# Snapping four kinds of pieces of a hand-written instruction order to the time steps of a triangular inverse, in a two-layer trunk on one core

## The chip, the core and the metric

The kernel runs on one core of a Trainium2 chip. A core has five engines with one in-order queue each: PE (TensorE, matrix products), DVE (VectorE), ACT (ScalarE), POOL (GpSimd) and SP (SyncE, which here issues nearly all DMAs). The metric is the device time of one execution in microseconds (us); lower is better. Times are medians of several executions. A profile is one further execution, recorded by the hardware profiler.

## The reference

Two layers are applied to 640 tokens (128 prompt tokens and 512 latent tokens, five blocks of 128) of width 1024. Layer A is a chunked gMLP mixer; layer B is a bidirectional gated DeltaNet with eight heads. All arithmetic is fp32. What the change touches is layer B:

```python
proj = h @ w_in                                   # q, k, v, the gate z, and the decay and beta columns
qkv = silu(short_conv(qkv, conv_w))
q = l2norm(q) * D_K ** -0.5 ; k = l2norm(k)
# per head and direction, chunks of tokens:
A = where(tril_strict, (k*beta) @ k.T * decay, 0)
u, w = triangular_solve(I + A, [v*beta, k*beta*exp(gcum)])
def step(S, ...):                                 # the scan over chunks
    v_new = u - w @ S
    o = (q*exp(gcum)) @ S + qk @ v_new
    S = S * exp(g_last) + k_dec.T @ v_new
o = o_forward + flip(o_backward)
o = o * rsqrt(mean(o**2) + eps) * norm_g
y = (o * silu(z)) @ w_out
```

## The kernel before

Layer B works head by head, and the work of several heads overlaps. Each kind of work is a Python generator that issues a few instructions and yields; what is issued between two yields is called a piece here. The kinds are:

- `project_head` and `project_z`: one 128-wide block of the projection, 17 pieces. A piece is one step of the contraction: three matrix products into the PSUM tile `pp` (lines 235, 236 and 237, since each fp32 operand is split into a high and a low part). They fill PE wherever nothing else is due. The weights' split is `whi` (a cast on ACT, line 230) and `wlo` (line 231).
- `conv`: the short convolution of one block (DVE line 848, tile `cacc`), ended by lines 851 (ACT) and 853 (DVE).
- `post_k`, `post_q`, `post_v`: after the convolution. `post_v` transposes v on PE (line 240) in two goes, four 128x128 blocks and then one, into the PSUM tile `px`, and ACT copies each to `nat` (line 938). `post_q` squares q on ACT and sums on PE against a column of ones (line 869).
- `chunk`: 40 pieces that build and invert the triangular matrices of one, two and two token blocks (three groups per head). PE products (lines 964, 1002, 1017, 1028, 1029, 1047, 1056, 1057, 1063, 1073) stand in every second piece from the seventh on, and in the piece after each a DVE or ACT instruction turns the PSUM result into the next operand: `TU` (lines 1004 on DVE, 1032 on ACT), `Y` (1022, DVE), `U` (1038, ACT), `T` (1050, ACT), `G` (1075, ACT), `A` and `M` (974, 982, DVE).
- `scan`: 24 pieces per head, one unit per direction and block. Products with the state `S` (line 1112, tile `ps`), then `r` on DVE (1115) and `o` on ACT (1118) or DVE (1120), then products with `G` (1125, 1126), then the new state and the sum `o` on DVE (1134, 1140).
- `norm_o`, `gate_z`: `gate_z` transposes the output `o` back on PE into `px` (line 240; four blocks and then one, for each of two halves of a head), and DVE multiplies it onto the gate `z` (line 1213).

`px` has one PSUM buffer, `ps` two, `pt` (the inverse's) three and `pp` two. A second tile in the only `px` buffer can be written once the reader of the first is done.

`stages` gives every piece list a start and an end in units of one head (about 80 us), and `turns` spreads its pieces evenly between them, sorts all pieces by time, and by place in the list where times are equal. The three groups of `chunk` start four of their own steps apart, and a step is `CSTEP / 4` = 0.0225 of a head, so that the inverse's pieces of all groups lie on one grid and the PE products of all three groups fall on the same steps. `scan` (24 pieces over a whole head), `post_q` (7), `post_v` (5) and `gate_z` (4) lie at times off this grid. PE and SP take their instructions exactly in this order (`manual_schedule`); the orders of DVE, ACT and POOL follow from it by a scheduler.

## Time and profile before

| what | value |
| --- | --- |
| median of 3 runs | 1356.4 us (1355.96 to 1357.52) |
| the profiled execution | 1356.03 us, of it the span from first to last instruction 1354.2 us |
| PE busy | 1282.5 us (95%) |
| DVE busy | 875.7 us (65%) |
| ACT busy | 578.7 us (43%) |
| POOL busy | 502.0 us (37%) |
| mean granted PE clock | 0.99 |

Layer B's loop over heads runs from about 505 us to 1245 us of the span, and layer B's output projection from there on. Numbers of a row in the timeline are its start and its length in us, then engine, line, operation, the tiles written and read, shapes and count; in square brackets stands how long the engine had been idle before it, and what ended that. Matmuls are pipelined: one starts before the modelled end of the one before it.

### The profile page before, as it was taken

How to read it: one execution, taken by the hardware profiler on the slowest of the kernel's cores; microseconds unless marked ns; L12 is line 12 of the kernel's file. 1: busy time of each engine (PE TensorE's matmuls, PEld its weight loads, DVE VectorE, ACT ScalarE, POOL GpSimd, SP SyncE). 2: the span in 40 equal slices, each digit the busy share in tenths (PEclk: the TensorE clock that was granted, in tenths of full speed). 3: DMA queues.
4: the chain of work that ended last, by engine and by line, in shares of the span. 5: the costliest groups of instructions: out<-in, count | busy, mean ns of one | idle time of the engine just before them, and what ended most of it. 6: DMA issues, size and time to landing. Idle time of an engine off the chain costs nothing. (4 is left out here: it accounts for less than half of the span.)

```text
span 1354.2 us, 22812 instructions
## 1 busy us (share of the span) xinstructions
PE 1282.5 (95%) x8773; PEld 1137.3 (84%) x8773; DVE 875.7 (65%) x1655; ACT 578.7 (43%) x1352; POOL 502.0 (37%) x503
## 2 busy tenths in 40 slices
PE   7999999999999999888999999999999999999996
PEld 4688999999997887778888898999899898887785
DVE  4654744444447566798677778686787868656357
ACT  2333522222224334665545354564545546443320
POOL 0221422222223434354343536355464646520024
PEclk9999999999999999998999999999999999999999
DMA  8512233333336324142122422234233242445732
GB/s 337 168 63 93 94 125 125 125 125 125 125 125 218 118 76 145 56 140 86 50 77 73 136 78 65 100 89 153 79 125 108 85 139 88 133 141 174 261 117 78
DMA packets 90254, 163.17 MB, mean 120 GB/s; under 512 B 9089, under 2 KB 55457, under 8 KB 90017
## 3 DMA queue, kind: packets, MB, share of 16 engines
q1 hardware_dynamic: 88704, 156.99, 35.3%
q10 hardware_dynamic: 1440, 4.72, 1.0%
q8 instruction: 69, 1.13, 0.3%
q14 instruction: 41, 0.33, 0.1%
HBM read 135.97 MB, written 25.71 MB: 119 GB/s over the span
## 5 line engine op out<-in xcount | busy, mean ns | idle before, releaser
L231 POOL TENSOR_TENSOR wlo<-wraw,whi 128x256 fp32r<-128x256 f32 (+1 forms) x188 | 194.4, 1054 | 261.6 <-ACT whi L230 261.6
L235 PE MATMUL pp<-hThi,whi 128*128 128x320 f32 (+1 forms) x784 | 280.1, 357 | 0.2 <-ACT hThi L230 0.2
L237 PE MATMUL pp<-hTlo,whi 128*128 128x320 f32 (+1 forms) x784 | 244.7, 312 | 0.4 <-POOL hTlo L231 0.4
L236 PE MATMUL pp<-hThi,wlo 128*128 128x320 f32 (+1 forms) x784 | 244.1, 311 | 0.0
L230 ACT CAST whi<-wraw 128x256 fp32r<-128x256 f32 (+1 forms) x262 | 143.5, 593 | 84.6 <-PE pacc L236 57.6
L235 PE MATMUL pacc<-hThi,whi 128*128 128x320 f32 x512 | 159.6, 312 | 0.0
L237 PE MATMUL pacc<-hTlo,whi 128*128 128x320 f32 x512 | 158.3, 309 | 0.0
L236 PE MATMUL pacc<-hThi,wlo 128*128 128x320 f32 x512 | 158.2, 309 | 0.0
L848 DVE SCALAR_TENSOR_TENSOR cacc<-xp,convw,cacc 128x642 f32<-128x642 f32 x128 | 137.7, 1076 | 25.0 <-ACT cacc L845 23.6
L235 PEld LDWEIGHTS pp<-hThi,whi 128*128 128x128 f32 (+1 forms) x784 | 148.8, 190 | 3.9 <-ACT hThi L230 0.3
L236 PEld LDWEIGHTS pp<-hThi,wlo 128*128 128x128 f32 (+1 forms) x784 | 148.6, 190 | 4.0
L237 PEld LDWEIGHTS pp<-hTlo,whi 128*128 128x128 f32 (+1 forms) x784 | 147.7, 188 | 1.8 <-POOL hTlo L231 0.7
L231 DVE TENSOR_TENSOR wlo<-wraw,whi 128x1024 fp32r<-128x1024 f32 (+1 forms) x74 | 87.7, 1196 | 60.0 <-ACT whi L230 59.5
L248 POOL TENSOR_TENSOR rs<-ve,mhalf 128x1 f32<-128x1 f32 (+2 forms) x39 | 40.1, 1028 | 170.1 <-DVE ve L246 166.7
L235 PEld LDWEIGHTS pacc<-hThi,whi 128*128 128x128 f32 x512 | 96.1, 188 | 3.1 <-issue 2.2
L236 PEld LDWEIGHTS pacc<-hThi,wlo 128*128 128x128 f32 x512 | 96.1, 188 | 0.0
L237 PEld LDWEIGHTS pacc<-hTlo,whi 128*128 128x128 f32 x512 | 96.1, 188 | 0.0
L256 POOL TENSOR_SCALAR gsq<-gsq 128x320 f32<-128x320 f32 (+1 forms) x52 | 27.7, 532 | 138.4 <-ACT gsq L255 137.4
L257 DVE TENSOR_TENSOR gsq<-pacc,gsq 128x320 f32<-128x320 f32 (+1 forms) x52 | 29.1, 565 | 73.9 <-POOL gsq L256 73.8
L255 ACT ACTIVATE gsq<-pacc 128x320 f32<-128x320 f32 (+1 forms) x52 | 25.7, 498 | 106.2 <-PE pacc L237 102.3
L235 PE MATMUL pacc<-whi,hThi 128*128 128x512 f32 x160 | 63.1, 406 | 7.6 <-ACT whi L230 4.4
L1032 ACT CAST TU<-pt 128x512 f16<-128x512 f32 (+1 forms) x120 | 57.2, 525 | 26.4 <-PE pt L1029 25.5
(333 smaller groups left out, 2974.9 us busy)
## 6 DMA issues: line engine op xcount, KB each, us to landing
wraw<-in_w_b SPq DMA_DIRECT2D x48, 512.0 KB
wraw<-in_w_ada SPq DMA_DIRECT2D x37, 512.0 KB
wraw<-in_w_uz SPq DMA_DIRECT2D x32, 512.0 KB
v<-kvd SPq DMA_DIRECT2D x72, 128.0 KB
wraw<-in_a_wo SPq DMA_DIRECT2D x16, 512.0 KB
wraw<-in_b_wo SPq DMA_DIRECT2D x16, 512.0 KB
kvd<-nat SPq DMA_DIRECT2D x24, 320.0 KB
cacc<-yd SPq DMA_DIRECT2D x24, 320.0 KB
```

The costliest lines, as they stand in the source:

```text
L230: self.nc.scalar.copy(hi, src)
L231: (e_lo or self.nc.vector).tensor_tensor(lo, src, f32(hi), op=ALU.subtract)
L235: mm(out, l_hi, r_hi, start=start, stop=False)
L236: mm(out, l_lo, r_hi, start=False, stop=False)
L237: mm(out, l_hi, r_lo, start=False, stop=stop)
L248: nc.gpsimd.tensor_tensor(r, ve, self.mhalf[:, 0:n], op=ALU.pow)
L255: nc.scalar.activation(sq, u, AF.Square)
L256: nc.gpsimd.tensor_scalar(sq, sq, GB, 1.0, op0=ALU.mult, op1=ALU.add)
L257: nc.vector.tensor_tensor(sq, u, sq, op=ALU.mult)
L848: nc.vector.scalar_tensor_tensor(acc, xp[:, i : i + PADN], w[:, i : i + 1], acc, op0=ALU.mult, op1=ALU.add)
L1032: nc.scalar.copy(part, p.rearrange("p s k t (j b) -> p s (k t j) b", b=b))
```

## The change

`turns` now moves the time of every piece of `scan`, `post_q`, `post_v` and `gate_z` to the middle of the step of the inverse's grid in which it lies. Two pieces of one list that fall into one step are issued directly after each other. At equal times the place in the list decides, so that `post_q` and `post_v` come first, then `scan`, then `chunk`, then `gate_z` (differences in the last digits of the times put it between two groups of `chunk` in places). The instructions themselves are the same. Lines of the changed kernel from `turns` on have numbers larger by 12.

```diff
@@ -83,6 +84,9 @@
           "post_q": 7, "post_v": 5, "gates": 7, "gates_e": 26, "residual": 17}
 
 
+SNAP = "scan", "post_q", "post_v", "gate_z"
+
+
 def stages():
 
 
@@ -131,7 +135,15 @@
 
 def turns(parts):
 
-    return sorted((f + (k + 0.5) / n * (t - f), i) for i, (_, _, n, f, t) in enumerate(parts)
+    step = CSTEP / 4
+
+    def when(name, at):
+
+        if name not in SNAP or at < 0:
+            return at
+        return math.floor(at) + (math.floor(at % 1.0 / step) + 0.5) * step
+
+    return sorted((when(name, f + (k + 0.5) / n * (t - f)), i) for i, (name, _, n, f, t) in enumerate(parts)
                   for k in range(n))
```

Three places in the orders show it. The first is PE while head 1 is scanned and head 2 is inverted: the second go of `post_v` (a transposed block of `cacc`) and the first go of `gate_z` (four blocks of `o`). Before:

```order
L240 MATMUL px_7657<-ident_487,cacc_7383 128x128
L235 MATMUL pp_7659<-hThi_64,whi_7482 128x320
L236 MATMUL pp_7659<-hThi_64,wlo_7483 128x320
L237 MATMUL pp_7659<-hTlo_65,whi_7482 128x320
L235 MATMUL pp_7659<-hThi_64,whi_7482 128x320
L236 MATMUL pp_7659<-hThi_64,wlo_7483 128x320
L237 MATMUL pp_7659<-hTlo_65,whi_7482 128x320
L240 MATMUL px_7673<-ident_487,o_6568 128x128
```

Changed:

```order
L249 MATMUL pp_7657<-hTlo_65,whi_7488 128x320
L252 MATMUL px_7661<-ident_487,cacc_7382 128x128
L252 MATMUL px_7670<-ident_487,o_6568 128x128
L252 MATMUL px_7670<-ident_487,o_6761 128x128
L252 MATMUL px_7670<-ident_487,o_6765 128x128
L252 MATMUL px_7670<-ident_487,o_6572 128x128
L247 MATMUL pp_7657<-hThi_64,whi_7488 128x320
```

Two pieces of projection that stood between the two uses of `px` now stand elsewhere, and the two follow each other directly. The second place is PE a little later, where the second half of `gate_z` transposes four blocks and then one. Before:

```order
L240 MATMUL px_7772<-ident_487,o_6568 128x128
L240 MATMUL px_7772<-ident_487,o_6767 128x128
L240 MATMUL px_7772<-ident_487,o_6771 128x128
L240 MATMUL px_7772<-ident_487,o_6572 128x128
L235 MATMUL pp_7752<-hThi_64,whi_7681 128x320
L236 MATMUL pp_7752<-hThi_64,wlo_7682 128x320
L237 MATMUL pp_7752<-hTlo_65,whi_7681 128x320
L1017 LDWEIGHTS A_1287_7451
L1017 MATMUL pt_7780<-TU_1311_7538,A_1287_7451 128x64
```

Changed:

```order
L252 MATMUL px_7783<-ident_487,o_6568 128x128
L252 MATMUL px_7783<-ident_487,o_6761 128x128
L252 MATMUL px_7783<-ident_487,o_6765 128x128
L252 MATMUL px_7783<-ident_487,o_6572 128x128
L252 MATMUL px_7789<-ident_487,o_6463 128x128
L1029 LDWEIGHTS A_1313_7555
L1029 MATMUL pt_7791<-TU_1337_7646,A_1313_7555 128x64
```

Before, two pieces of projection and ten products of line 1017 stood between the four blocks and the one (the fence ends before the second piece); now nothing does. The third place is ACT near the end of the inverse of head 5, where the cast `T` (line 1050) stands among the four casts of the next block of weights. Before:

```order
L834 COPY xp_765_4886<-pp_11545 128x320
L230 CAST whi_11772<-wraw_11448 128x256
L845 ACTIVATE cacc_11659<-xp_765_4886,convw_4867 128x642
L1050 CAST T_2196_11663<-pt_11642 128x512
L230 CAST whi_11772<-wraw_11448 128x256
L912 COPY kq_11454<-px_11676 128x4x128
L230 CAST whi_11772<-wraw_11448 128x256 x2
```

Changed:

```order
L846 COPY xp_765_4886<-pp_11545 128x320
L242 CAST whi_11777<-wraw_11448 128x256
L857 ACTIVATE cacc_11662<-xp_765_4886,convw_4867 128x642
L242 CAST whi_11777<-wraw_11448 128x256 x3
L1062 CAST T_2200_11672<-pt_11642 128x512
L924 COPY kq_11454<-px_11682 128x4x128
```

Three casts of weights that stood behind `T` now stand ahead of it.

## The prediction

> **What bounds the kernel now.** I read the page's head first, then stretches of layer B, then what PE waits for, then the timeline around those waits.

> ```profile
> span 1354.2 us, 22812 instructions
> 735.00:810.00 75.00, 72.97 (x582) 67.92 (x583) 55.95 (x121) 39.28 (x111) 33.75 (x40) 1.00 0.29 91
> PE px L240 <- DVE cacc L853: 8.0, 4, 4.4
> PE pt L1047 <- ACT U L1038: 4.6, 6, 1.6
> PE ps L1112 <- DVE o L1140: 3.9, 5, 1.2
> PE pt L1029 <- DVE Y L1022: 3.2, 5, 0.6
> PE pp L237 <- DVE wlo L231: 0.5, 1, 0.5
> ```

> The second row is a stretch of 75 us in the middle of layer B (busy time of PE, weight loads, DVE, ACT and POOL; granted clock; DMA). PE works 73 of 75 us at full clock, DVE 56, ACT 39. PE sets the pace, so two things move the time: how long PE's own stream takes, and where PE stands still. The last rows are recorded waits of PE: total, times, longest. They recur about once a head.

> The change keeps every instruction and moves it, so the cost is read from the orders: which products follow which on PE, and how much PE work lies between a product and the DVE, ACT or DMA result that it needs.

> **Term 1: fewer switches of PE's stream.**

> ```profile
> L235 PE MATMUL pp<-hThi,whi 128*128 128x320 f32 (+1 forms) x784 | 280.1, 357 | 0.2 <-ACT hThi L230 0.2
> L236 PE MATMUL pp<-hThi,wlo 128*128 128x320 f32 (+1 forms) x784 | 244.1, 311 | 0.0
> 849.17 0.31 PE L235 MATMUL pp<-hThi,whi 128*128 128x320 f32 x1
> 844.08 0.39 PE L235 MATMUL pp<-hThi,whi 128*128 128x320 f32 x1
> 837.29 0.50 PE L235 MATMUL pp<-hThi,whi 128*128 128x320 f32 x1
> ```

> Line 235 opens each projection piece and is 46 ns longer in the mean than line 236 of the same size. The timeline rows show why: 0.31 us inside a run of pieces, 0.39 after transposes (fp16 products read the same), 0.50 after the scan's fp32 products. A return to the projection costs 0.08 or about 0.18 us. Counted in PE's order over layer B's loop, a run of projection pieces begins 343 times before and 293 times in the changed kernel: after fp32 products 125 and 97, after transposes 72 and 51, after fp16 products 137 and 136. Saved: 28 x 0.18 + 22 x 0.08 = 6.8 us where PE is what sets the time. It is not everywhere: term 2 shows a stretch at each head's start where DVE does, and two of the saved fp32 switches (0.36) lie in it; one more (0.16) lies just ahead of the wait on `Y` (line 1029). Over five heads 2.6 us of the 6.8 turn into waiting. Term 1 is -4.2 us.

> [...]

> **Term 2: the wait of line 1112 goes, and mostly comes back.**

> ```profile
> 833.51 2.61 DVE L982 SCALAR_TENSOR_TENSOR M<-pe,beta,masks 128x128 f32<-128x128 f32 x2
> 836.05 0.41 DVE L1140 TENSOR_TENSOR o<-o,ps 128x256 f32<-128x256 f32 x1
> 836.38 0.91 DVE L982 SCALAR_TENSOR_TENSOR M<-pe,beta,masks 128x128 f32<-128x128 f32 x1
> 836.51 1.13 PE L1112 MATMUL ps<-S,kq 128*128 128x256 f32 x4 [0.71 <-DVE o L1140]
> 837.21 0.41 DVE L1004 TENSOR_TENSOR TU<-pt,wm 128x256 f16<-128x256 f32 x1
> 837.92 0.23 PE L1017 MATMUL pt<-TU,A 128*128 128x64 f16 x2
> ```

> The second `ps` tile is free only when DVE has done line 1140, which stands behind three of the inverse's `M` instructions. The changed order of DVE has 1140 ahead of `ge`, `pe`, `A` and `M`, so this wait of 0.71 us goes. But DVE's total work up to `TU` is the same, and line 1017 needs `TU`, which is done at 837.62; PE used it at 837.92. PE can gain those 0.30 less the 0.06 that it takes to start: 0.24 us in each of five heads, -1.2 us. All of the 3.9 us in the list would go if DVE were also earlier: that end is kept for the range.

> **Term 3: later transposes of v.**

> ```profile
> PE px L240 <- DVE cacc L853: 0.8, 1, 0.8
> ```

> This is the wait list of 1110 to 1200 us. There, and at 679 us (the 4.4 in the first fence), the first go of `post_v` waits for its convolution. The snap moves one projection piece ahead of it in each. A piece takes 0.44 us (from 849.17, quoted above, to the transposes at 849.61, quoted below): -0.8 us.

> **Terms 4 and 5: two uses of the only `px` buffer meet.**

> ```profile
> 841.54 0.27 PE L240 MATMUL px<-ident,cacc 128*128 128x128 f32 x1
> 841.74 0.44 ACT L1199 ACTIVATE z<-pp 128x320 f32<-128x320 f32 x1 [0.29 <-PE pp L237]
> 842.07 0.27 ACT L938 ACTIVATE nat<-px 128x128 f32<-128x128 f32 x1
> 842.52 0.60 PE L240 MATMUL px<-ident,o 128*128 128x128 f32 x4
> 849.61 0.60 PE L240 MATMUL px<-ident,o 128*128 128x128 f32 x4
> 850.25 0.75 DVE L1213 SCALAR_TENSOR_TENSOR z<-px,ngT,z 128x512 f32<-128x512 f32 x1 [0.84 <-PE px L240]
> 851.33 0.27 PE L240 MATMUL px<-ident,o 128*128 128x128 f32 x1
> ```

> Now the copy to `nat` and the product onto `z` run beside projection pieces. In the changed order nothing lies between the two uses, in six heads each. First pair: `nat` ends at 842.34, so the gate's transposes could start at 842.40, where an unbroken stream would start them 0.11 after the block before, at 841.65: 0.75 us. ACT was 0.26 late there because of line 1199, so I take 0.65 between 0.5 and 0.85: 6 x 0.65 = +3.9 us. Second pair: DVE ends at 851.00, the single block could start at 851.05, and an unbroken stream would start it at 850.05: 1.0 us, where nothing excludes more, since in some heads one or two `Y` stand ahead of line 1213 on DVE. The sixth head already waits there. 5 x 1.0 + 0.8 = +5.8 us. Behind the waiting transposes stand a group of the inverse's products and all projection pieces; nothing on PE can pass.

> **Term 6: ACT gets `T` and `U` later.**

> ```profile
> 1046.93 0.57 ACT L1050 CAST T<-pt 128x512 f16<-128x512 f32 x1
> 1048.18 0.72 ACT L230 CAST whi<-wraw 128x256 fp32r<-128x256 f32 x2
> 1047.67 0.23 PE L1056 MATMUL pt<-T,A 128*128 128x128 f16 x1
> 888.59 0.22 PE L1056 MATMUL pt<-T,A 128*128 128x128 f16 x1
> 887.00 0.57 ACT L1050 CAST T<-pt 128x512 f16<-128x512 f32 x1
> S<-in_state SPq DMA_DIRECT2D x16, 128.0 KB
> v<-kvd SPq DMA_DIRECT2D x72, 128.0 KB
> 1048.38 0.86 SPq L1092 DMA_DIRECT2D S<-in_state  x2
> 1051.85 0.69 ACT L985 ACTIVATE M<-kn,scal 128x128 f32<-128x128 f32 x2 [1.90 <-DMA kn<-kvd]
> 1053.82 0.40 PE L1047 MATMUL pt<-id,U 128*128 128x128 f16 x4 [0.83 <-ACT U L1038]
> ```

> Three casts of weights now stand ahead of `T`. Two take 0.72 us, so three take 1.0. `T` ended at 1047.50 and PE used it at 1047.67, so 0.8 us are lost there; in two heads it is so, in two others `T` had 1.0 us to spare (887.57 against 888.59), in a third some 0.3 are lost. On SP the two loads of `S` and one of `v` now go ahead of `ex` and `kn` (0.86 us of issue for `S` alone, and 3 x 128 KB in the same queue). For `kn` that counts: ACT waits 1.90 us for it at 1051.85, and behind it stand the tanh of line 851 and `U`, for which PE waits 0.83 us already. A delay of `kn`, which I bound by nothing (it may have to wait for its own data anyway) and 1.9 us (that same wait once more), goes there in part, and `U` now stands ahead of one copy. I take 1.3 us in two heads, 0.3 in three, casts and `kn` together, since PE that is late by the casts waits less for `U`: +3.5 us.

> **Term 7: cover lost under line 1032.**

> ```profile
> 946.74 1.89 PE L1112 MATMUL ps<-S,kq 128*128 128x256 f32 x8
> 947.45 1.05 ACT L1032 CAST TU<-pt 128x512 f16<-128x512 f32 x2
> 949.78 0.46 PE L1017 MATMUL pt<-TU,A 128*128 128x64 f16 x10
> ```

> In each head one such burst of the scan moves from behind the inverse's products 1028 and 1029 to ahead of them (eight products and the dearer switch behind them, 1.7 us in all), and only three projection pieces (1.3 us) are left for ACT's three casts. Here `TU` was done at 948.50, 1.28 us before its use, so 0.4 us of new waiting; by the same reckoning hardly 0.1 in five other heads, and 0.4 in the first, where four casts of weights come ahead of `TU` too: +1.0 us, between 0 and 2.

> **The sum.** -4.2 - 1.2 - 0.8 + 3.9 + 5.8 + 3.5 + 1.0 = +8.0 us. A PE that stands still lets DVE and ACT catch up, so of the waits that follow in the same head (on `Y` 3.2 over five, on `U` 4.6 over six) some go: I take 0.4 in five heads, 2 us. Net +6.0 on a profiled execution of 1356.03 us (its span and 1.8 around it, not in the span); the median of the runs is 1356.4, which gives 1362.4 us. POOL's order changes by single places of the weights' low parts; PE's recorded wait on them is 0.5 us in all, so I cost it at nothing; were that cover gone, a block's low part late by one instruction would cost as much again. SP's later loads of `v` keep their places.

> **The rivals.** (a) Faster: DVE is not what sets line 1017, and stalls at `px` are repaid in full. Then terms 1 to 3 are -6.8 - 3.9 - 0.8 = -11.5, terms 4 and 5 stay at +9.7 and give back 1.2 us in five heads, and terms 6 and 7 vanish: -7.8, or 1348.6. For it speaks that the waits at lines 1029 and 1047 are set by other engines; against it, that DVE is busy without a gap from 833.5 to 837.6. It decides once what `px` costs, net of what is given back, is under 8.8 us (11.5 less 2.7) while terms 6 and 7 stay near zero. Chance 0.18. (b) No change that can be told: term 6 vanishes since ACT, busy half the time, takes the casts early, and 3 us are repaid: 1358.5. Chance 0.2. (c) More: each of the four new waits a head delays evacuation and weights as well, term 1 is eaten wholly by waits: 1368. Chance 0.1. [...] Chance 0.02. That the order does not change is excluded by the rows quoted with the change.

> **The numbers.** My case, 1359.1 to 1366, has 0.5. A difference under 0.2% (2.7 us) can't be told from none. The range reaches to 1354 and 1370: with term 2 at -3.9 and term 6 at zero the sum is 1356.2, and a little of (a) is taken in; with `nat` at 0.85, `kn` at its full 1.9 us in two heads and term 7 at 2 it comes near the upper end. Slower 0.62, the same 0.2, faster 0.18.

> **What would show it.** In the changed profile: line 235's mean under 357 ns; line 1112's wait on 1140 gone and one of line 1017 on `TU` of 1004 (0.7 us a head) in its place; line 240 waiting for ACT `nat` (0.5 us, six times) and for DVE `z` (0.85, six times); line 1056 waiting for `T`; line 1047's wait on `U` longer. It is wrong if the `px` waits are absent or repaid, or if DVE's `TU` comes earlier.

## The result, and the profile after

The changed kernel takes 1373.6 us (median of 4 runs, 1371.7 to 1377.4) against 1356.2 us: a ratio of 1.0127, interval 1.0104 to 1.0150, slower by 17.2 us by the ratio. Slower was forecast, but by 6 us. The profiled execution took 1371.66 us, its span is 15.7 us longer than before. Line numbers are now larger by 12.

First the head of the page, the line that opens a projection piece, and from the list of what PE waits for (total, times, longest) the rows that the argument uses. The first row is of the kernel before, the others are of the changed one.

```profile
PE pt L1017 <- DVE TU L1004: 4.1, 2, 2.6
span 1369.9 us, 22824 instructions
L247 PE MATMUL pp<-hThi,whi 128*128 128x320 f32 (+1 forms) x784 | 272.1, 347 | 0.2 <-ACT hThi L242 0.2
PE pt L1029 <- DVE TU L1016: 13.9, 7, 4.1
PE px L252 <- DVE cacc L865: 7.0, 3, 4.2
PE pt L1059 <- ACT U L1050: 6.2, 7, 1.8
PE px L252 <- DVE z L1225: 5.8, 7, 1.1
PE pt L1041 <- DVE Y L1034: 3.6, 6, 0.6
PE pt L1040 <- DVE Y L1034: 2.5, 2, 1.6
PE px L252 <- ACT nat L950: 2.2, 6, 0.4
```

The wait on `o` is gone, as forecast. The wait for `TU`, which had 4.1 us, has 13.9: the largest single item, where a small return was forecast. Both `px` waits are there, in six heads each (a seventh wait for `z`, 0.21 us, belongs to no such pair). Line 247's mean fell by 10 ns (357 to 347), and its busy time by 8.0 us over 784 products (280.1 to 272.1), near the 6.8 us of term 1, and the time did not fall with it.

Next the place of that wait in the head that the prediction showed. DVE and PE, before (first fence, besides the rows shown under term 2) and after:

```profile
830.51 1.09 DVE L853 SCALAR_TENSOR_TENSOR cacc<-xp,cacc 128x642 f32<-128x642 f32 x1 [0.47 <-ACT xp L851]
831.53 0.41 DVE L967 TENSOR_TENSOR ge<-pt,ex 128x256 f32<-128x256 f32 x1
833.25 0.34 DVE L982 SCALAR_TENSOR_TENSOR M<-pe,beta,masks 128x128 f32<-128x128 f32 x1
834.77 1.03 PE L1112 MATMUL ps<-S,kq 128*128 128x256 f32 x4
```

```profile
830.51 1.04 DVE L865 SCALAR_TENSOR_TENSOR cacc<-xp,cacc 128x642 f32<-128x642 f32 x1 [0.47 <-ACT xp L863]
832.06 0.42 DVE L1152 TENSOR_TENSOR o<-o,ps 128x256 f32<-128x256 f32 x1 [0.39 <-ACT r L1143]
832.40 0.42 DVE L979 TENSOR_TENSOR ge<-pt,ex 128x256 f32<-128x256 f32 x1
834.11 4.03 DVE L994 SCALAR_TENSOR_TENSOR M<-pe,beta,masks 128x128 f32<-128x128 f32 x4
838.07 0.41 DVE L1016 TENSOR_TENSOR TU<-pt,wm 128x256 f16<-128x256 f32 x1
835.00 1.89 PE L1124 MATMUL ps<-S,kq 128*128 128x256 f32 x8
838.53 0.22 PE L1029 MATMUL pt<-TU,A 128*128 128x64 f16 x2 [1.64 <-DVE TU L1016]
```

By chance both profiles have the last convolution of DVE (lines 853 and 865) start at 830.51, so the rows can be laid side by side. Before, `ge` followed it directly and `TU` was done at 837.62. After, DVE stands 0.39 us for `o`, which now comes ahead of `ge`, and `TU` is done at 838.48: 0.86 later. Not all of that is `o`: up to the start of `ge`, and without the 0.34 that `o` takes in either order, 0.53 are lost, and the four `M` products take 3.96 us from start to start (834.11 to 838.07) where they took 3.63 (833.25 to 836.05 and 836.38 to 837.21). Why `M` is slower, no run isolates. PE starts line 1029 at 838.53, where it started at 837.92. It stood 1.64 us where it had stood 0.71 on `o`: 0.61 of the difference is DVE's, the other 0.32 is PE work (a projection piece, set against other small moves) that lay ahead of this point and now lies behind it. Five heads wait like this, 1.5 to 1.7 us each, 8.1 in all. The longest wait, 4.1 us in the last head where it was 1.45, is of another order: before, DVE had `ge`, `pe` and `A` ahead of its last convolution; now it stands 0.87 us for `xp`, does that convolution, and only then the chain to `TU`:

```profile
1162.45 1.11 DVE L865 SCALAR_TENSOR_TENSOR cacc<-xp,cacc 128x642 f32<-128x642 f32 x1 [0.87 <-ACT xp L863]
1170.50 0.22 PE L1029 MATMUL pt<-TU,A 128*128 128x64 f16 x2 [4.11 <-DVE TU L1016]
```

Next the two places at `px`, after:

```profile
842.89 0.28 ACT L950 ACTIVATE nat<-px 128x128 f32<-128x128 f32 x1
843.22 0.66 PE L252 MATMUL px<-ident,o 128*128 128x128 f32 x4 [0.37 <-ACT nat L950]
852.11 0.75 DVE L1225 SCALAR_TENSOR_TENSOR z<-px,ngT,z 128x512 f32<-128x512 f32 x1
852.91 0.33 PE L252 MATMUL px<-ident,o 128*128 128x128 f32 x1 [0.84 <-DVE z L1225]
```

They are as the prediction drew them. A recorded wait counts from the modelled end of the product before it, which lies behind the point where the next could start (in the rows above one transpose takes 0.33 us, four take 0.66 together); I put each stall at 0.2 to 0.3 us more than the bracket says (an estimate from the starts of unbroken streams).

### The profile page after: what moved, and what is told of

It reads as the page before. It is cut to its first block, busy times and chain, and to the rows that moved or that the text cites. A ratio compares the mean times of both kernels' runs of the same rounds, so it can differ in the third digit from the quotient of the medians.

```text
span 1369.9 us, 22824 instructions
## 1 busy us (share of the span) xinstructions
PE 1284.1 (94%) x8773; PEld 1136.5 (83%) x8773; DVE 880.2 (64%) x1655; ACT 579.7 (42%) x1352; POOL 499.4 (36%) x503
## 3 DMA queue, kind: packets, MB, share of 16 engines
q8 instruction: 69, 1.13, 0.3%
## 5 line engine op out<-in xcount | busy, mean ns | idle before, releaser
L247 PE MATMUL pp<-hThi,whi 128*128 128x320 f32 (+1 forms) x784 | 272.1, 347 | 0.2 <-ACT hThi L242 0.2
L860 DVE SCALAR_TENSOR_TENSOR cacc<-xp,convw,cacc 128x642 f32<-128x642 f32 x128 | 134.1, 1048 | 22.8 <-ACT cacc L857 21.3
L243 DVE TENSOR_TENSOR wlo<-wraw,whi 128x1024 fp32r<-128x1024 f32 (+1 forms) x74 | 90.5, 1236 | 59.0 <-ACT whi L242 58.5
L260 POOL TENSOR_TENSOR rs<-ve,mhalf 128x1 f32<-128x1 f32 (+2 forms) x39 | 40.1, 1028 | 175.5 <-DVE ve L258 172.1
L1034 DVE TENSOR_TENSOR Y<-pt,wm 128x128 f16<-128x128 f32 (+1 forms) x144 | 47.8, 372 | 34.1 <-PE pt L1029 34.1
## 6 DMA issues: line engine op xcount, KB each, us to landing
v<-kvd SPq DMA_DIRECT2D x72, 128.0 KB
```

Of the source, the lines that this page charges most:

```text
L243: (e_lo or self.nc.vector).tensor_tensor(lo, src, f32(hi), op=ALU.subtract)
L247: mm(out, l_hi, r_hi, start=start, stop=False)
L260: nc.gpsimd.tensor_tensor(r, ve, self.mhalf[:, 0:n], op=ALU.pow)
L860: nc.vector.scalar_tensor_tensor(acc, xp[:, i : i + PADN], w[:, i : i + 1], acc, op0=ALU.mult, op1=ALU.add)
L1034: nc.vector.tensor_tensor(yc, pair(p), pair(self.wm[:, l - 1, :, 0:nt]), op=ALU.mult)
```

## The experiments

All timed kernels, with the ratio to the kernel before of the same chip. The last four columns are of one profile each: its span, all waits of PE in it added up, the time lost to a lower granted clock (one minus the clock, over rows of 10 us), and what is left of the span without these two. The profiled run need not be a typical one: for scan_alone, flips_alone and m_after_tu it was the slowest of five or six.

| kernel | median us | ratio, interval | span | waits | clock | rest |
| --- | --- | --- | --- | --- | --- | --- |
| before | 1355.6 to 1356.2 | 1 | 1354.2 | 61.2 | 13.3 | 1279.7 |
| the change | 1373.6 | 1.0127, 1.0104 to 1.0150 | 1369.9 | 75.4 | 11.8 | 1282.6 |
| scan_alone | 1365.2 | 1.0071, 1.0046 to 1.0095 | 1371.8 | 69.8 | 20.9 | 1281.0 |
| flips_alone | 1374.9 | 1.0138, 1.0115 to 1.0162 | 1374.7 | 73.2 | 19.6 | 1281.9 |
| post_v_alone | 1363.8 | 1.0054, 1.0038 to 1.0069 | 1357.2 | 66.7 | 8.1 | 1282.4 |
| gate_alone | 1364.6 | 1.0081, 1.0060 to 1.0102 | 1362.3 | 67.4 | 11.3 | 1283.6 |
| gates_later | 1370.9 | 1.0112, 1.0090 to 1.0133 | 1368.0 | 74.4 | 14.1 | 1279.4 |
| gates_apart | 1364.1 | 1.0066, 1.0046 to 1.0087 | 1360.4 | 69.0 | 11.4 | 1280.1 |
| m_after_tu | 1365.2 | 1.0075, 1.0057 to 1.0092 | 1367.0 | 69.5 | 14.8 | 1282.7 |
| apart_and_m | 1358.5 | 1.0022, 1.0004 to 1.0040 | 1360.1 | 65.2 | 15.5 | 1279.4 |
| m_after_tu_before | 1355.4 | 0.9997, 0.9983 to 1.0011 | 1353.6 | 61.3 | 9.9 | 1282.4 |
| scan_and_m | 1361.5 | 1.0052, 1.0036 to 1.0068 | 1361.0 | 63.0 | 17.9 | 1280.1 |
| scan_behind | 1377.9 | 1.0168, 1.0144 to 1.0192 | 1379.0 | 72.9 | 27.8 | 1278.3 |

The rest is 1278 to 1284 us whatever the order, without a trend that follows the time: nearly every difference is waiting or clock. Part of the `px` stalls, which the brackets don't record, is in it where the pairs meet.

**Does a switch cost anything?**

```python
for other in (full, turn, half):      # 2 fp32 products, 4 transposes, 4 fp16 products
    for _ in range(24): proj()        # 3 products of 128x320
    for _ in range(24): other()
    for _ in range(24):
        proj(); other()
```

> This kernel leaves out the whole trunk. PE alone runs 24 rounds of three projection-like products (fp32r, 128x320) and of two fp32 products of 128x256, first each kind in one block, then alternating; then the same with four fp32 transposes and with four fp16 products of 64 columns. Same products in both, only the number of switches differs (24 round trips more). Theory of the prediction (a return to the projection costs 0.18 us after fp32, 0.08 after transposes and fp16): the alternating stretch is longer by 24 x 0.18 = 4.3 us with fp32 and by 24 x 0.08 = 1.9 us with transposes and with fp16. Theory from the two traces (start to start, a switch costs nothing after fp32 and transposes; the first product of a run only starts earlier behind its forerunner and so looks longer): under 0.3 us longer with fp32 and transposes, with fp16 perhaps 24 x 0.065 = 1.6 us.

The timeline of PE (each row one block; the 48 fp32 products have 96 records, x96):

```profile
49.86 20.88 PE L1341 MATMUL px<-raw 128*128 128x256 f32 x96
70.39 0.79 PE L1337 MATMUL pp<-hr 128*128 128x320 f32 x3
...
101.67 10.91 PE L1337 MATMUL pp<-hr 128*128 128x320 f32 x72
112.41 10.64 PE L1345 MATMUL px<-ident,raw 128*128 128x128 f32 x96
122.81 0.69 PE L1337 MATMUL pp<-hr 128*128 128x320 f32 x3
...
143.90 10.80 PE L1337 MATMUL pp<-hr 128*128 128x320 f32 x72
154.54 2.97 PE L1349 MATMUL px<-h 128*128 128x64 f16 x96
157.35 0.69 PE L1337 MATMUL pp<-hr 128*128 128x320 f32 x3
...
173.04 0.69 PE L1337 MATMUL pp<-hr 128*128 128x320 f32 x3
```

From start to start: 72 projection products take 10.74 us (101.67 to 112.41) and later 10.64. With fp32, in blocks 20.53 + 10.74 = 31.27, alternating 101.67 - 70.39 = 31.28: nothing for 24 switches there and back. With transposes 10.40 + 10.74 = 21.14 against 21.09: nothing. With fp16, 2.81 + 10.64 = 13.45 against 15.69: 0.093 us for each. So the theory of the prediction's term 1 falls for fp32 and transposes, and holds in size for fp16, whose switches the change left alone (137 and 136). This is one run. Its granted clock is 1.00 from 10 to 50 us and 0.96 in the mean of 50 to 190; the last row shown ends at 173.73, and since equal blocks agree within 0.1 us (10.74 and 10.64) I put the lower clock behind it (an estimate). The longer duration of a first product (0.79 us for three after fp32, 0.69 after fp16) is no guide to its price: after fp32 and transposes it goes with an early start behind its forerunner and costs nothing from start to start.

**One part alone.**

```diff
-SNAP = "scan", "post_q", "post_v", "gate_z"
+SNAP = ("scan",)             # scan_alone
+SNAP = "post_v", "gate_z"    # flips_alone
+SNAP = ("post_v",)           # post_v_alone
+SNAP = ("gate_z",)           # gate_alone
```

> Only scan is moved to the steps; the flips (post_v, gate_z) and post_q stay at their times, so the two uses of the px buffer stay apart. Theory 1 (no gain from fewer switches; DVE's chain from the products of line 976 to TU of line 1016 runs later since the sum o of line 1152 now stands ahead of it): the wait on o at line 1124 goes (3.9 us), line 1029 waits for TU 1.6 us a head, no wait for z of line 1225; +5 to +7 us against before, about 1362. Theory 2 (the prediction's terms 1, 2, 6, 7 without the px pairs): -4.2 -1.2 +3.5 +1.0 -2, about 1353.5.

Measured +9.6 us (1365.2 against 1355.6): theory 2, the prediction's own sum without the pairs, falls, and theory 1 was too low. PE's waits are as it said:

```profile
PE pt L1029 <- DVE TU L1016: 13.8, 7, 4.0
PE px L252 <- DVE z L1225: 0.7, 2, 0.5
```

The waits are 8.6 us above before; the mean clock of the six runs is 0.984 to 0.989, where before has 0.989 to 0.994 in its eleven.

> Only post_v and gate_z are moved; scan and post_q stay. Theory 1: the two uses of px meet as in the full change, in six heads each; waits of about 0.37 us (nat) and 0.85 to 1.0 us (z) a head by the trace, and some 0.3 us more a head that the trace does not record as waiting; nothing is repaid: +9 to +11 us, about 1366. The wait on o of line 1152 stays. Rival: PE's standstill is repaid at the next waits (on Y, U, o): +4 us or less, about 1360.

Measured +19.3 us by the medians (18.7 by the ratio), nearly twice theory 1. `px` is as expected, but it is not all:

```profile
PE ps L1124 <- DVE o L1152: 7.2, 5, 1.6
PE px L252 <- DVE z L1225: 5.8, 7, 1.1
PE px L252 <- ACT nat L950: 2.5, 6, 0.6
```

The wait on `o`, which the full change removes, has grown here from 3.9 to 7.2. The next two runs take the two flips apart.

> Only post_v is moved. gate_z stays at its times, so the pairs at px do not meet except in one head. The four transposes of v (0.43 us) go from ahead of the scan's burst (line 1124) to behind it in each head, and with them work that covered DVE's chain to o and TU. Theory 1 (PE work that moves from ahead of that wait to behind it is lost in full): the wait on o at line 1124 grows from 0.7 to 1.4 us a head, +3 to +5 us against before, about 1359.5. Rival (moving a transposition by a step costs nothing, all of the loss of flips_alone is px): 1355 to 1357.

Measured +7.7 us by the medians (1363.8 against 1356.1; 7.3 by the ratio), above theory 1 and well above its rival. The wait on `o` is 7.2 us in the list, 1.4 in four heads as expected; at 679 us a wait of 3.5 us of line 1124 has taken the place of the 4.4 for the convolution. The transposes of v moved from ahead of the burst to behind it, and the 0.43 us that they covered is paid in full and a little more (0.7 us a head). The profiled execution, 1359.0 us, is 3.0 above before's, with 5.5 more of waits, 2.7 of rest and 5.2 less of clock; the other runs lie up to 1367.7, at clocks down to 0.985.

> Only gate_z is moved. The second pair at px (four blocks of o, then one) meets in six heads; the first pair does not, one projection piece lies between. Theory 1: the wait for z of line 1225, 5 us, and some 1.5 us that is not recorded as waiting, +6 to +8 us against before, about 1363; lines 1124 and 1029 wait as before. With post_v_alone (+7.3) it leaves about 4 of the 18.7 us of flips_alone for the first pair. Rival (px repaid later): +2 us.

Measured +8.9 us by the medians, 11.0 by the ratio (8.1 to 13.8). Waits for `z` are 5.8 us, those on `o` 3.9 and so unchanged: the second pair alone, as theory 1 has it, but dearer. With post_v_alone that leaves 2.7 us of flips_alone for the first pair by the medians and 0.4 by the ratios, where about 4 were expected: the price of the first pair stays loose.

**Taking the pairs apart.**

```diff
# gates_later
+        late = 1 if name == "gate_z" else 0
-        ... (math.floor(at % 1.0 / step) + 0.5) * step
+        ... (math.floor(at % 1.0 / step) + late + 0.5) * step
# gates_apart
+        if name == "gate_z":
+            return when(name, f + 0.5 / n * (t - f)) + (k + 1) * step
```

> The full change, but gate_z goes one step (0.0225 of a head) later than its step, so that no two uses of px follow each other directly. Theory 1 (losses add): the px waits go and the time falls by 9 to 11 us against the full change, to about 1363; the wait of line 1029 on TU stays at 1.6 us a head. Rival (the px stalls only delay what would wait for TU or U anyway): about 1371, with longer waits on TU or U.

The edit did not do what its expectation says: two pieces of the gate's second half still fell into one step, and only the first pair came apart. It measured 2.0 us under the full change by the ratios, but the two intervals overlap, and 5.1 us for `z` are still in the list. So it bears on the first pair alone, whose waits (2.2 us) are gone while those for DVE's copy to `nat` grew by 2.0, and says nothing on the second.

> The full change, but the pieces of gate_z lie on consecutive steps, from one step after their first piece's own: at least two projection pieces lie between any two uses of px (in gates_later the four blocks and the one of the gate's second half still followed each other directly). Theory 1: both px waits (nat 2.2, z 5.1 us over before) and some 3 us that the trace does not record as waiting go: 8 to 10 us under the full change, about 1364; what is left over before, about 9 us, is the scan's part. Rival (standstill at px is repaid at the next wait): under 4 us better, 1370 or more.

Measured 1364.1, the number of theory 1: 8.3 us under the full change by the ratios (0.0061 of 1356). The wait of the transposes for `z` is gone from the list (that for DVE's `nat` grew from 3.4 to 5.2 us, that for `TU` from 13.9 to 16.0; those on `U` and `Y` fell by 0.9 each). All waits together fell by 6.4 us where 8.0 went at `px`, so a small part of a stall is repaid, and the rival (repaid at the next wait) falls.

**DVE's chain.** The four `M` products of a group stand ahead of the first group's `TU`; they go two pieces later.

```diff
         M = t(b1, [P, nt, 4, P], F32, f"M{nt}")
         yield
-        for i, c in enumerate(cs): ... M[:, i, 1 + d] ...
         yield
         A16 = ... ; L16 = ...
         yield
+        for i, c in enumerate(cs): ... M[:, i, 1 + d] ...
         yield
```

> The full change, with the four M products of a group (DVE line 994, about 1.0 us each) issued two of the inverse's steps later, so that most of them stand behind the first group's TU (line 1016) on DVE. Theory 1 (at the head's start DVE's queue, not PE, sets the time, and what stands on DVE ahead of TU is paid by PE): TU is 2 to 4 us earlier, line 1029's wait of 1.6 us a head goes, and the time falls by 6 to 10 us against the full change, to 1364 to 1368. Rival (the M products are only moved in front of Y, line 1034, or T, and PE waits there instead): 1371 to 1375, with longer waits of lines 1040 and 1041 on Y.

Measured 1365.2: 7.1 us under the full change by the ratios. In the five steady heads two of the four `M` products went behind `TU`; the wait of line 1029 fell from 13.9 us to 0.2, in one head. The rival has a share: line 1040's wait on `Y` grew from 2.5 to 5.6 us and that for `z` from 5.8 to 8.2.

> The kernel before with the same later M products. Theory 1: the wait of line 1112 on o goes (3.9 us in five heads) together with the waits of line 1017 on TU (2.6 and 1.5), with Y unchanged: 3 to 6 us faster than before, about 1351. Rival (Y or r comes later by what the M products take): no difference or slower by 2 us.

No difference, where 3 to 6 us were expected: a miss, and no test of theory 1. In the five steady heads the edit left DVE's order as it was: three `M` products, `o`, the fourth `M`, `TU`. So the wait on `o` is 4.0 us as before. Only around the first two heads and in the last did `M` go behind `TU`; the 3.6 us gained there came back at line 1028 on `Y` (1.8 to 3.4) and elsewhere. The waits are 61.3 us against 61.2.

> The full change with both cures: gate_z on consecutive steps as in gates_apart, and the M products two steps later as in m_after_tu. Theory 1 (two separate places, their costs add): 1373.4 less 9.0 (1373.1 to 1364.1) less 8 (to 1365.2), about 1357, level with before within 3 us; neither px after z nor line 1029 after TU waits over 0.5 us a head. Rival (both stalls delay the same engine, so curing one cures part of the other): 1361 or more.

Measured 1358.5, +3.0 us by the ratio: 14.2 of the 17.2 us are undone, and 8.3 + 7.1 = 15.4 were to be expected if the two add. Within the intervals the two costs add, as theory 1 has it. Its forecast for the waits fails: `TU` kept 4.9 us, 0.9 to 1.0 in three of the later heads and 1.9 in the last. The full change thus loses at two places, and the two cures bring it back near, but not below, the kernel before.

> Only scan is moved to the steps, and the M products stand behind TU. Theory 1: o of line 1152 is early, so line 1124 does not wait (3.9 us in before), TU is early, so line 1029 does not wait (4.1 in before), px and post_v are as before: 3 to 5 us faster than before, about 1352. Rival (line 1059's wait on U and line 1040's on Y take it back, or the scan's burst moved ahead of the inverse's products loses cover elsewhere): 1355 to 1359.

A miss: +7.0 us by the ratio instead of -4. Two steady heads are 78.6 and 78.9 us long between their first products of line 976 against 79.5 and 79.4 before, 0.7 less in the mean, as theory 1 said; of the three behind them two are longer (82.3 against 80.5, 82.5 against 79.7), at a clock of 0.98 each. The waits, 63.0 us, are near before's, and the clock costs 4.6 us more.

> Only scan is moved, to three quarters of the step instead of its middle, so that its pieces come behind those of the inverse: on DVE the sum o of line 1152 (1153 here) stands behind ge, pe, A and M, and DVE does not idle for it ahead of ge. Theory 1 (in scan_alone the idle time for o ahead of ge, 0.33 to 0.39 us, and its 0.4 us shift DVE's chain to TU, and the rest of the TU wait is cover that moved): TU is 0.4 to 0.8 us earlier than in scan_alone but o 4 us later, so the wait moves to line 1124 (1125 here); the time lies between before and scan_alone, about 1360. Rival (only the position of the scan's products on PE counts): as scan_alone, 1365.

Another miss: 1377.9, slower than scan_alone.

```profile
846.63 0.41 DVE L1017 TENSOR_TENSOR TU<-pt,wm 128x256 f16<-128x256 f32 x1
847.10 0.22 PE L1030 MATMUL pt<-TU,A 128*128 128x64 f16 x2 [2.62 <-DVE TU L1017]
848.10 1.89 PE L1125 MATMUL ps<-S,kq 128*128 128x256 f32 x8
```

`o` no longer holds up `ge`, and `TU` is done 6.4 us after the last convolution (it ends at 840.69 there), 0.6 earlier than with the full change (6.9), as expected. But the whole burst of the scan (four products, eight rows, 1.7 us) went behind line 1030, and the wait is 2.62 us. Both halves of the reading show here: DVE sets the end of this stretch (PE starts 0.06 us behind `TU`), and the PE work moved behind it is lost (the wait is 2.62 us where it was 0.71 on `o` before).

**The clock.** In the table the granted clock costs up to 14.5 us more than before (27.8 less 13.3). Read in rows of 1 us over the loop, in before, the full change and scan_behind, it is 0.50 for 3.4, 6.8 or 10.2 us at a time. In the layer B loop of the full change such stretches begin at 608.2, 676.5, 980.3 and 1171.4 us: within 1 us behind waits of 2.5, 1.85 and 4.1 us, and the second inside one of 4.2. A kernel with nothing but that, run once:

```python
for rep in range(4):
    for n in (64, 512, 1024, 2048, 4096):
        ...                           # DVE copies as long as n elements, between two PE blocks
        for _ in range(45): proj()    # 135 products, some 20 us
```

> This kernel leaves out the whole trunk. PE alone runs blocks of 135 projection-like products (some 20 us); between two blocks it waits for a chain of DVE copies of five lengths (about 0.9 to 5 us), four rounds of the five. Theory 1 (PE's standstill itself brings the stretches of halved granted clock that the traces show behind some waits, 3.4 us each, 1.7 us lost): such stretches begin within 2 us behind most of the waits over 1.5 us and behind none of the shortest, and the blocks behind them are 1.7 us longer. Rival (the halved stretches come from elsewhere, from heat, power or other engines' work in the full kernel): granted clock 1.00 in all blocks once PE is warm, whatever the wait.

```profile
103.84 20.07 PE L1337 MATMUL pp<-hr 128*128 128x320 f32 x135 [1.23 <-DVE hr L1349]
125.86 21.62 PE L1337 MATMUL pp<-hr 128*128 128x320 f32 x135 [1.96 <-DVE hr L1349]
150.89 21.45 PE L1337 MATMUL pp<-hr 128*128 128x320 f32 x135 [3.41 <-DVE hr L1349]
...
237.42 20.08 PE L1337 MATMUL pp<-hr 128*128 128x320 f32 x135 [1.95 <-DVE hr L1349]
260.91 22.64 PE L1337 MATMUL pp<-hr 128*128 128x320 f32 x135 [3.41 <-DVE hr L1349]
...
372.11 21.60 PE L1337 MATMUL pp<-hr 128*128 128x320 f32 x135 [3.41 <-DVE hr L1349]
...
482.26 21.33 PE L1337 MATMUL pp<-hr 128*128 128x320 f32 x135 [3.41 <-DVE hr L1349]
```

```profile
226.00:236.00 10.00, 9.46 (x65) 9.20 (x63) 0.47 (x2) 0.00 (x0) 0.00 (x0) 1.00 0.00 0
260.00:264.00 4.00, 3.09 (x11) 3.10 (x12) 0.82 (x2) 0.00 (x0) 0.00 (x0) 0.50 0.00 0
```

A block takes 20.07 us. Behind all four waits of 3.41 us it took 1.3 to 2.6 us longer, behind one of the four of 1.96 us 1.55, behind none of the twelve of 0.73 to 1.23. The second fence shows the granted clock (third number from the end) around two waits: 1.00 ahead of the end of the one of 1.95 us at 237, 0.50 from just ahead of the end of the one of 3.41 us at 260.9. The five stretches begin at 126.6, 150.6, 259.8, 372.5 and 481.7 us, three of them while PE still waited. Theory 1 holds here, with a softer edge than it said: of the four waits of 1.96 us, one was followed by a stretch.

## Why the prediction was right in its sign and wrong in its size

By its own terms, on the profiles (before to after):

| term | forecast | measured |
| --- | --- | --- |
| 1 switches | -4.2 | 0: the rest of the span is 1279.7 and 1282.6; 0.00 us a switch by switch_cost after fp32 and transposes |
| 2 `o` goes, `TU` comes | -1.2 | -3.9 + 9.8 = +5.9: +4.2 in the five heads that it counted, +1.7 in two others |
| 3 later transposes of v | -0.8 | -1.0 (8.0 to 7.0) |
| 4 and 5 pairs at `px` | +9.7 | +2.2 + 5.1 recorded, some 3 more in the rest: about 10; 8.3 less with the pairs apart |
| 6 `T`, `U`, casts | +3.5 | +0.7 on `U` (4.6 and 0.9 on DVE's part, to 6.2); no wait for `T` |
| 7 cover under line 1032 | +1.0 | no wait for ACT's `TU` |
| caught up later | -2.0 | +1.1: the waits on `Y` grew (5.0 to 6.1) |
| clock | none | -1.5 in this profile |

The measured column adds up to about 15, the spans differ by 15.7.

**The step that failed first is term 1, by 4.2 us.** I read the longer duration of a first projection product as its price. In the traces products overlap, and a duration that begins earlier is longer without costing anything; the steps from start to start would have shown it in the trace of before: after fp32, 0.03 us to the first product and 0.33 to the next, against 0.22 and 0.15 in unbroken streams, the same sum within 0.01 us. switch_cost has no price for these switches after fp32 and transposes (31.28 against 31.27 us, 21.09 against 21.14); what makes them free, no run isolates. With term 1 at zero, to which the prediction gave a chance of 0.02, the forecast is 1362.4 + 4.2 = 1366.6, still 7 us under the result.

**Term 2 had the right place and a wrong size, by 7 us, and is the larger miss.** I took DVE's work up to `TU` as unchanged and gave PE 0.24 us a head. DVE's chain became 0.86 us longer: `o`, put ahead of `ge`, has to be waited for (0.39 of DVE's idle time, which `M` hid before) and the `M` products took 0.33 longer, for a reason that no run isolates. I also did not count which PE work passed from ahead of this point to behind it, and DVE's new order in the last head (a wait of 4.1 us for 1.45) isn't in the term at all. post_v_alone and scan_behind show how much that decides: 0.4 and 1.7 us of PE work moved a head, and 0.7 and 1.9 us more waiting than before.

Terms 3, 4 and 5 came out as drawn, and gates_apart shows that little of the `px` stalls is repaid. Terms 6 and 7 were together 3.8 us too high: PE came later to these places too. In the two heads where `T` had 0.17 us to spare it had 0.9 in the changed kernel, although three casts now stand ahead of it. The 2 us of catching up were not there. Rival (a) fails on both of its conditions: DVE does set line 1017, and `px` is not repaid in full. Rival (c), 1368, came nearest in its number, but its reason (term 1 is earned and then eaten by waits) isn't what the runs show: that term was never there.

The mean clock of the runs of the full change, 0.988 to 0.991, may hold 2 or 3 us of the median against before's 0.989 to 0.994 (an estimate); the profile shows none of it. That part isn't settled. Nor is it why m_after_tu gains 7.1 us in the full change, while the same edit with scan alone (scan_and_m) gains 2.6; the clock, of which scan_and_m loses 17.9 us in its profile, can hold a part of that.

## What to carry to other kernels

Price an order on an in-order engine from start to start, never from the durations of overlapped instructions. Where another engine sets the end of a stretch, find the first product that needs its result, and count the work ahead of it: here, what a move took from ahead to behind was paid in full (0.43 us of work cost 0.7 in post_v_alone, 1.7 us cost 1.9 in scan_behind), and so were the instructions that came ahead of that result on the other engine (`TU` 0.86 us later, 0.61 of it waited for by PE). Two uses of a single buffer that a tidy order puts next to each other cost the wait for its reader each time here (0.37 us for `nat` and 0.84 for `z` in the head shown). And read the order that a scheduler makes of an edit before you count on it: m_after_tu_before changed nothing in five of its heads.

## What the hardware showed unexpectedly

```profile
1170.00:1175.00 5.00, 4.50 (x24) 4.14 (x24) 4.02 (x12) 1.64 (x5) 2.36 (x3) 0.66 0.11 37
```

That is behind the wait of 4.1 us for `TU`, which ended at 1170.5: the clock is 0.50 from 1171.41 to 1174.82, for 3.41 us.

The length of the wait doesn't decide it alone. The five stretches of clock_after_wait begin 24.0, 109.2, 112.7 and 109.2 us apart, within 0.2 us 7, 32, 33 and 32 times 3.41; the four in the loop of the full change 68.3, 303.8 and 191.1, which is 20, 89 and 56 times 3.413. So I cut both traces into intervals of 3.413 us, counted from the start of such a stretch. The four waits of 1.96 us put 1.96, 1.49, 1.90 and 0.99 us into one interval, and only the first was followed by a halved one. In the loop of the full change every interval at full clock with 1.85 us or more of PE standing still (1.85, 2.47, 2.50 and 2.55) was followed by a halved one, and none with up to 1.81. The edge isn't sharp across the two kernels (1.90 without such a stretch, 1.85 with one), and one stretch in the trace of before (at 1054.2 us, behind an interval with 0.83 us) doesn't fit. The same wait of 1.96 us thus cost 1.55 us more once and nothing three times. Whether that explains part of the spread between runs of one kernel was not tested; what sets the clock, no run isolates.
